# Banded attention inside a mixed layer: the low part of q on all 128 rows, and the softmax division on GpSimd

## The chip, the cores and the metric

One Trainium2 chip, one core. The metric is the device time of one execution in microseconds (us). TensorE is called PE below, its weight loads PEld, VectorE DVE, ScalarE ACT, GpSimd POOL, SyncE SP.

## The reference, cut to what matters

The whole block is a norm, an input projection, a linear recurrence beside a banded attention, an output projection, a cross attention over 256 memory rows, and a routed mixture of 32 experts. The change lies in the banded attention alone, which works on 2048 tokens, 8 heads of 64, each chunk of 64 queries seeing its own and the 8 chunks before:

```python
scores = jnp.einsum('bnqhd,bnkhd->bhnqk', qc, kb, preferred_element_type=jnp.float32)
scores = scores * (ATT_HEAD_DIM ** -0.5) + rel_bias_band(rel_bias).astype(jnp.float32)[None, :, None]
scores = jnp.where(valid[None, None, :, None, :], scores, NEG_INF)
probs = jax.nn.softmax(scores, axis=-1).astype(v.dtype)
out = jnp.einsum('bhnqk,bnkhd->bnqhd', probs, vb)
```

## The kernel before, in words

`front` (L646) computes the first half of the block, `phase2` the cross attention and the routing, `moe` the experts. `front` runs over 4 column groups `c` (two heads each) and, inside, over 4 blocks `t` of 512 tokens: 16 steps. All matrix products are done on pairs: each operand is split into a rounded part and the rest, and `mm3` (L54, L56 to L58) issues three matmuls for one product.

One call of `step` (L363) makes five projections of a block, in the order xr, xg, q, k, v (`run(0)` to `run(4)`; `proj`, L354, 24 matmuls of 128x512 each). After each 12 matmuls it calls `fill(i)`, i from 0 to 9, which runs the pieces of work that hang in slot i. Between the projections stands the recurrence: two gate products, a chain of ACT and DVE operations, and at its end the product `yr` (L425), its store (L426), its square (L561), the addition to a partial sum loaded from memory (L565) and the store of that (L566), these five on POOL.

The pieces in the slots are the attention of the step before (`attention`, L452). It has 8 units: 2 heads times 4 query tiles j of 128 queries. A unit's `scores` (L477) hangs in slot i, its `transp` (L501) in slot i+3, and for every second unit `out` (L516) in slot i+5; the last ones spill over into the slots 0 to 2 of the next step, `done` (L541) among them, which stores the attention's output and squares it on POOL.

In `scores` a unit's 640 keys lie in two parts of n1 and n2 columns, one from the block before and one from this block; in the first block of a column group there is only the second part, of 128 to 512 columns. For each part two matmuls add into the score tile `sc`: L486 with `qhh`, the rounded q twice on 128 rows, against `kst`, which holds rounded k on rows 0 to 63 and the rest of k on rows 64 to 127; and L487 with `qlo`, the rest of q on 64 rows, against the first 64 rows of `kst`. Then DVE adds the bias and takes the maximum (L490), ACT takes the exponential with its sum (L495), DVE the reciprocal of the sum (L497) and the product of the row with it (L498). `transp` turns the result on PE (L510) into `ptp`, from which ACT (L513) and DVE (L514) make the pair `PT`; `out` multiplies it with v (L534). `sc` and `ptp` have one buffer each.

`qhh` and `qlo` are made in `step` from the projection's PSUM tile `pq`: for each of two heads two ACT copies (L435, L436) and one DVE operation (L437). The projections share two PSUM buffers (`psA`), so the v projection (`run(4)`) writes where the q projection stood. Both engines read `pq`, and in the trace the second head's first copy waits for the first head's L437, of whose output it reads nothing.

The framework orders the instructions of each engine when the program is built; where the trace's order differs from the code's, that is its doing. POOL's queue also holds, in the last block of a column group, the splitting of the next group's weights (L342, L343), and in the first column group half of the splitting of h (L162).

Of the kernel before, what the change touches and what calls it, by code (L numbers as in the profile page):

```python
# [11 lines left out]
F32R = mybir.dt.float32r  # L12
# [4 lines left out]
ALU = mybir.AluOpType  # L17
# [9 lines left out]
TB = 512  # L27
# [18 lines left out]
def f32(ap):  # L46
    return ap.bitcast(F32)


class K:  # L50
# [312 lines left out]
    def step(self, c, t, st, wts, gh, gl, fill, h):  # L363

        nc = self.nc
        pt2 = self.pt2
        T2 = lambda name, dt=F32: pt2.tile([P, TB], dt, name=name, tag="t2")
        cnt = [0]

        def run(g):  # L370
            r = None
            for r in self.proj(wts[g], h):
                fill(cnt[0])
                cnt[0] += 1
            return r

        pxr = run(0)
        xre = self.p2.tile([P, TB + 3], F32, name="xre")
        if t == 0:
            nc.vector.memset(xre[:, 0:3], 0.0)  # L380
        else:
            nc.vector.tensor_copy(xre[:, 0:3], st["xre"][:, TB:TB + 3])
        nc.scalar.copy(xre[:, 3:], pxr)
        st["xre"] = xre
        cw = lambda i: self.col("convw", c * 4 + i)
        xc = T2("xc")
        nc.scalar.activation(xc, pxr, AF.Identity, scale=cw(3), bias=self.col("convb", c))
        for i in range(3):
            nc.vector.scalar_tensor_tensor(xc, xre[:, i:i + TB], cw(i), xc, op0=ALU.mult, op1=ALU.add)
        xch = T2("xch", F32R)  # L390
        xcl = T2("xcl", F32R)
        nc.scalar.copy(xch, xc)
        nc.vector.tensor_sub(xcl, xc, f32(xch))
        pxg = run(1)
        xg = T2("xg_half")
        nc.scalar.mul(xg, pxg, 0.5)
        th = []
        for gi in range(2):
            pg = self.psM.tile([P, TB], F32, name="pg", tag="m")
            self.mm3(pg, gh[:, gi], gl[:, gi], xch, xcl, True, True)  # L400
            tt = T2(f"th{gi}")
            nc.scalar.activation(tt, pg, AF.Tanh, scale=0.5, bias=self.hb[:, 4 * gi + c:4 * gi + c + 1])
            th.append(tt)
        kc_ = self.Kc[:, c:c + 1]
        av = T2("av")
        nc.scalar.activation(av, th[0], AF.Exp, scale=kc_, bias=kc_)
        tl_ = T2("tl")
        nc.scalar.activation(tl_, th[0], AF.Tanh, scale=kc_, bias=kc_)
        a2 = T2("a2")
        nc.scalar.activation(a2, av, AF.Square)  # L410
        g2 = T2("g2")
        nc.scalar.activation(g2, xg, AF.Square, scale=2.0)
        nc.vector.scalar_tensor_tensor(a2, a2, 1.0, tl_, op0=ALU.add, op1=ALU.mult)
        nc.vector.tensor_scalar(g2, g2, 0.044715, 1.0, op0=ALU.mult, op1=ALU.add)
        nc.vector.tensor_mul(g2, g2, xg)
        nc.scalar.activation(g2, g2, AF.Tanh, scale=2.0 * 0.7978845608028654)
        nc.scalar.activation(a2, a2, AF.Sqrt, scale=-0.25)
        nc.vector.scalar_tensor_tensor(xc, th[1], 1.0, xc, op0=ALU.add, op1=ALU.mult)
        nc.vector.tensor_mul(xc, xc, a2)
        hs = T2("hs")  # L420
        nc.vector.tensor_tensor_scan(hs, av, xc, 0.0 if t == 0 else st["h"][:, TB - 1:TB], op0=ALU.mult, op1=ALU.add)
        st["h"] = hs
        nc.vector.scalar_tensor_tensor(g2, g2, 1.0, xg, op0=ALU.add, op1=ALU.mult)
        yr = T2("yr")
        nc.gpsimd.tensor_tensor(yr, g2, hs, op=ALU.mult)  # L425
        nc.gpsimd.dma_start(out=self.yT[t][:, c], in_=yr)  # L426
        self.acc_sq(0, t, c, yr)

        pq = run(2)
        qst = []  # L430
        for hd in range(2):
            sl = slice(64 * hd, 64 * hd + 64)
            qhh = T2(f"qhh{hd}", F32R)
            qlo = pt2.tile([64, TB], F32R, name=f"qlo{hd}", tag="t2")
            nc.scalar.mul(qhh[0:64], pq[sl], 0.125)  # L435
            nc.scalar.mul(qhh[64:128], pq[sl], 0.125)  # L436
            nc.vector.scalar_tensor_tensor(qlo, pq[sl], 0.125, f32(qhh[0:64]), op0=ALU.mult, op1=ALU.subtract)  # L437
            qst.append((qhh, qlo))
        st["q"] = qst
        pk = run(3)  # L440
        for hd in range(2):
            sl = slice(64 * hd, 64 * hd + 64)
            kt = self.r3.tile([P, TB], F32R, name=f"kst{hd}")
            nc.scalar.copy(kt[0:64], pk[sl])
            nc.vector.tensor_sub(kt[64:128], pk[sl], f32(kt[0:64]))
            st[("k", t, hd)] = kt
        pv = run(4)
        vt = T2("vt")
        nc.scalar.copy(vt, pv)
        st["vt"] = vt  # L450

    def attention(self, c, t, st, bias):  # L452

        nc = self.nc
# [17 lines left out]
        def dims(j):  # L472
            n1 = 0 if t == 0 else (4 - j) * P
            n2 = (j + 1) * P
            return n1, n2, n1 + n2

        def scores(hd, j):  # L477
            qhh, qlo = qst[hd]
            qs = slice(j * P, (j + 1) * P)
            n1, n2, n = dims(j)  # L480
            sc = self.psS.tile([P, 1024], F32, name="sc")
            parts = [(sc[:, 512:512 + n2], kcur[hd][:, 0:n2])]
            if n1:
                parts.append((sc[:, 512 - n1:512], kprev[hd][:, j * P:TB]))
            for o, kk in parts:
                nc.tensor.matmul(o, qhh[:, qs], kk, start=True, stop=False)  # L486
                nc.tensor.matmul(o, qlo[:, qs], kk[0:64], start=False, stop=True)  # L487
            pr = self.r4.tile([P, 640], F32, name="st")
            mx = self.sm.tile([P, 1], F32, name="mx")
            nc.vector.tensor_tensor_reduce(pr[:, 0:n], sc[:, 512 - n1:512 + n2], bias[hd][:, 640 - n:640], 1.0, -3e38,  # L490
                                           op0=ALU.add, op1=ALU.max, accum_out=mx)
            nm = self.sm.tile([P, 1], F32, name="nm")
            nc.vector.tensor_scalar_mul(nm, mx, -1.0)  # L493
            ls = self.sm.tile([P, 1], F32, name="ls")
            nc.scalar.activation(pr[:, 0:n], pr[:, 0:n], AF.Exp, bias=nm, accum_out=ls)  # L495
            rl = self.sm.tile([P, 1], F32, name="rl")
            nc.vector.reciprocal(rl, ls)  # L497
            nc.vector.tensor_scalar_mul(pr[:, 0:n], pr[:, 0:n], rl)  # L498
            live[(hd, j)] = pr

        def transp(hd, j):  # L501
# [45 lines left out]
        for i, (hd, j) in enumerate(units):  # L547
            slots[i].append(lambda hd=hd, j=j: scores(hd, j))
            slots[i + 3].append(lambda hd=hd, j=j: transp(hd, j))
            if j % 2 == 1:  # L550
                slots[i + 5].append(lambda hd=hd, j=j: out(hd, j // 2))
# [542 lines left out]
    def moe(self):  # L1094
        nc, tc, a = self.nc, self.tc, self.a
        with ExitStack() as ctx:
# [259 lines left out]
            def unit(blks, ahead=(), last=None):  # L1356
# [40 lines left out]
                if not one:  # L1397
                    def mid(q):
                        if q == 1:
                            htrans(blks[0])  # L1400
                        step(1)
                        w.split()
                    hmid(blks[1], gu(blks[1], u, mid))
                    down(blks[0], d, put, lambda: (step(1), w.split()), False)
                    step(1)
                else:
                    w.split(2)
# [187 lines left out]
```

## Time and profile before

| what | value |
|---|---|
| device time, median of 3 runs | 2418.55 us (2418.11 to 2421.62) |
| the profiled execution | 2420.44 us |
| its span, first to last instruction | 2418.7 us |
| PE busy | 2298.4 us, 95% |
| DVE busy | 1572.8 us, 65% |
| ACT busy | 1351.3 us, 56% |
| POOL busy | 478.7 us, 20% |

The profile's page gives busy times and the costliest groups of instructions over the whole span. Its slices of the span show how busy each engine is over time, and the clock granted to TensorE. Busy time of PE is modelled for pipelined matmuls (a matmul's row lasts longer than the distance to the next one), so how fast PE works is read from the starts of its matmuls in the timeline.

### The profile page before, as it was taken

How to read it: one execution, taken by the hardware profiler on the slowest of the kernel's cores; microseconds unless marked ns; L12 is line 12 of the kernel's file. 1: busy time of each engine (PE TensorE's matmuls, PEld its weight loads, DVE VectorE, ACT ScalarE, POOL GpSimd, SP SyncE). 2: the span in 40 equal slices, each digit the busy share in tenths (PEclk: the TensorE clock that was granted, in tenths of full speed). 3: DMA queues.
4: the chain of work that ended last, by engine and by line, in shares of the span. 5: the costliest groups of instructions: out<-in, count | busy, mean ns of one | idle time of the engine just before them, and what ended most of it. 6: DMA issues, size and time to landing. Idle time of an engine off the chain costs nothing. (4 is left out here: it accounts for less than half of the span.)

```text
span 2418.7 us, 33205 instructions
## 1 busy us (share of the span) xinstructions
PE 2298.4 (95%) x11312; PEld 1868.2 (77%) x11312; DVE 1572.8 (65%) x3072; ACT 1351.3 (56%) x2300; POOL 478.7 (20%) x500
## 2 busy tenths in 40 slices
PE   8999999999999999999999999699999999999993
PEld 7766777787777778887888888577888777877782
DVE  7668766766776775435444444676777777777774
ACT  7677556555655664324343333466666667666654
POOL 1333521321241220000111111111212112121120
PEclk9999999999999999999999999799999999999997
DMA  8865642443334344633111111688998999989967
GB/s 329 297 233 177 216 156 105 144 176 121 133 125 167 121 141 140 200 109 131 53 64 60 62 53 60 230 277 292 301 309 281 307 298 297 310 275 307 298 207 307
DMA packets 160961, 475.83 MB, mean 197 GB/s; under 512 B 25393, under 2 KB 40370, under 8 KB 159506
## 3 DMA queue, kind: packets, MB, share of 16 engines
q1 hardware_dynamic: 129186, 369.92, 43.3%
q0 software_dynamic: 30448, 99.54, 13.5%
q10 hardware_dynamic: 1152, 4.19, 0.6%
q8 instruction: 90, 1.47, 0.2%
q14 instruction: 85, 0.70, 0.1%
HBM read 379.57 MB, written 98.99 MB: 198 GB/s over the span
## 5 line engine op out<-in xcount | busy, mean ns | idle before, releaser
L1141 DVE TENSOR_TENSOR w_hl<-w_raw,w_hl 128x1024 fp32r<-128x1024 f32 x384 | 458.9, 1216 | 120.3 <-ACT w_hl L1140 118.4
L1140 ACT CAST w_hl<-w_raw 128x1024 fp32r<-128x1024 f32 x384 | 388.9, 1049 | 143.9 <-DMA w_raw<-in_up_dram 35.0
L1209 PE MATMUL pg<-w_hl,xh 128*128 128x512 f32 x1120 | 355.9, 399 | 1.1 <-ACT xh L1198 1.1
L56 PE MATMUL pp<-h_hl,w_hl 128*128 128x512 f32 x640 | 264.4, 415 | 2.0 <-ACT h_hl L161 1.0
L58 PE MATMUL pp<-h_hl,w_hl 128*128 128x512 f32 x640 | 251.7, 394 | 2.9 <-DVE w_hl L340 2.9
L57 PE MATMUL pp<-h_hl,w_hl 128*128 128x512 f32 x640 | 251.9, 394 | 1.6 <-DVE h_hl L162 0.9
L1209 PEld LDWEIGHTS pg<-w_hl,xh 128*128 128x128 f32 x1120 | 205.6, 189 | 42.6 <-ACT xh L1198 1.5
L1209 PE MATMUL pg<-w_hl,xl 128*128 128x512 f32 x560 | 219.9, 393 | 0.0
L1272 PE MATMUL py<-w_hl,hth 128*128 128x512 f32 x560 | 143.9, 400 | 23.0 <-ACT hth L1255 23.0
L1259 POOL DMA_INDIRECT acc_d<-ys,ti x46 | 85.3, 1854 | 385.2 <-ACT ys L1276 371.6
L56 PEld LDWEIGHTS pp<-h_hl,w_hl 128*128 128x128 f32 x640 | 120.3, 188 | 37.9 <-issue 9.2
L1272 PEld LDWEIGHTS py<-w_hl,hth 128*128 128x128 f32 x560 | 106.3, 192 | 51.6 <-ACT hth L1255 29.7
L58 PEld LDWEIGHTS pp<-h_hl,w_hl 128*128 128x128 f32 x640 | 120.5, 188 | 30.5 <-DVE w_hl L340 3.3
L495 ACT ACTIVATE st<-st,nm 128x640 f32<-128x640 f32 (+4 forms) x128 | 97.3, 761 | 80.2 <-DVE nm L493 79.6
L57 PEld LDWEIGHTS pp<-h_hl,w_hl 128*128 128x128 f32 x640 | 120.9, 189 | 25.3 <-POOL h_hl L162 2.5
L514 DVE TENSOR_TENSOR PT<-ptp,PT 128x640 fp32r<-128x640 f32 (+4 forms) x128 | 94.1, 735 | 51.5 <-ACT PT L513 51.1
L1209 PEld LDWEIGHTS pg<-w_hl,xl 128*128 128x128 f32 x560 | 105.5, 188 | 23.2
L490 DVE CUSTOM_DVE_ANT_0 st<-sc,bias 128x640 f32<-128x640 f32 (+4 forms) x128 | 94.3, 737 | 38.5 <-PE sc L487 36.7
L1178 POOL DMA_INDIRECT xs<-h_d,ti x48 | 59.4, 1238 | 294.3 <-PE px L1189 129.1
L56 PE MATMUL sc<-At,xh 128*128 128x512 f32 x256 | 103.7, 405 | 1.3 <-ACT xh L830 1.3
L498 DVE TENSOR_SCALAR st<-st,rl 128x640 f32<-128x640 f32 (+4 forms) x128 | 102.7, 802 | 3.1
L1209 PE MATMUL pg<-w_hl,xr 128*128 128x512 f32 x416 | 102.4, 393 | 0.0
(389 smaller groups left out, 5151.8 us busy)
## 6 DMA issues: line engine op xcount, KB each, us to landing
w_raw<-in_gate_dram SPq DMA_DIRECT2D x128, 512.0 KB
w_raw<-in_up_dram SPq DMA_DIRECT2D x128, 512.0 KB
w_raw<-in_down_dram SPq DMA_DIRECT2D x128, 512.0 KB
h_hl<-hT SPq DMA_DIRECT2D x96, 512.0 KB
hT<-h_hl POOLq DMA_DIRECT2D x32, 512.0 KB, 6.4
w_raw<-in_w_in_dram SPq DMA_DIRECT2D x40, 256.0 KB
xr<-in_x_dram SPq DMA_DIRECT2D x32, 256.0 KB
xt<-in_xT_dram SPq DMA_DIRECT2D x32, 256.0 KB
```

Of the source, the lines that this page charges most:

```text
L56: mm(ps, lh, rh, start=start, stop=False)
L57: mm(ps, lh, rl, start=False, stop=False)
L58: mm(ps, ll, rh, start=False, stop=stop)
L490: nc.vector.tensor_tensor_reduce(pr[:, 0:n], sc[:, 512 - n1:512 + n2], bias[hd][:, 640 - n:640], 1.0, -3e38, op0=ALU.add, op1=ALU.max, acc ...
L495: nc.scalar.activation(pr[:, 0:n], pr[:, 0:n], AF.Exp, bias=nm, accum_out=ls)
L498: nc.vector.tensor_scalar_mul(pr[:, 0:n], pr[:, 0:n], rl)
L514: nc.vector.tensor_sub(PT[:, 1, s0:s0 + nb], src, f32(PT[:, 0, s0:s0 + nb]))
L1140: nc.scalar.copy(wt[:, 0], raw)
L1141: nc.vector.tensor_sub(wt[:, 1], raw, f32(wt[:, 0]))
L1209: nc.tensor.matmul(pg, x[:, k], wt[:, l, cs], start=(k == 0 and i == 0), stop=(k == KC - 1 and i == np_ - 1))
L1259: nc.gpsimd.indirect_dma_start(out=self.acc_d, in_=ys[0:b.n], in_offset=None, compute_op=op, out_offset=bass.IndirectOffsetOnAxis(ap=b.ti[ ...
L1272: nc.tensor.matmul(o, h[:, k], m[k][:, l, nn * TB:(nn + 1) * TB], start=(j == 0), stop=(j == len(ps) - 1))
```

## The change

The low part of q is written to both halves of 128 rows, by two DVE operations for a head where there was one, in the order ACT, DVE, ACT, DVE. The second matmul of a score part contracts over 128 rows, with the whole of `kst`; so the product of the low part of q with the low part of k, which was left out, is added. The product of the exponentials with the reciprocal of their sum moves from DVE to POOL.

```diff
             qhh = T2(f"qhh{hd}", F32R)
-            qlo = pt2.tile([64, TB], F32R, name=f"qlo{hd}", tag="t2")
-            nc.scalar.mul(qhh[0:64], pq[sl], 0.125)
-            nc.scalar.mul(qhh[64:128], pq[sl], 0.125)
-            nc.vector.scalar_tensor_tensor(qlo, pq[sl], 0.125, f32(qhh[0:64]), op0=ALU.mult, op1=ALU.subtract)
+            qlo = T2(f"qlo{hd}", F32R)
+            for o in (slice(0, 64), slice(64, 128)):
+                nc.scalar.mul(qhh[o], pq[sl], 0.125)
+                nc.vector.scalar_tensor_tensor(qlo[o], pq[sl], 0.125, f32(qhh[0:64]), op0=ALU.mult, op1=ALU.subtract)
...
                 nc.tensor.matmul(o, qhh[:, qs], kk, start=True, stop=False)
-                nc.tensor.matmul(o, qlo[:, qs], kk[0:64], start=False, stop=True)
+                nc.tensor.matmul(o, qlo[:, qs], kk, start=False, stop=True)
...
             nc.vector.reciprocal(rl, ls)
-            nc.vector.tensor_scalar_mul(pr[:, 0:n], pr[:, 0:n], rl)
+            nc.gpsimd.tensor_scalar(pr[:, 0:n], pr[:, 0:n], rl, None, op0=ALU.mult)
```

## Rows read from the trace of the kernel before

**Rows 1.** Busy time of the engines by stretch; each engine's number of instructions in brackets.
```profile
core 0: us, PE busy (x) PEld busy (x) DVE busy (x) ACT busy (x) POOL busy (x), PEclk, DMA share, GB/s
150.00:407.40 257.40, 250.13 (x1198) 193.58 (x1198) 188.41 (x402) 165.38 (x321) 84.69 (x100) 0.99 0.50 180
407.40:850.00 442.60, 442.60 (x2184) 348.75 (x2182) 301.98 (x636) 257.80 (x467) 121.92 (x129) 1.00 0.39 137
...
457.70:508.00 50.30, 50.30 (x253) 39.56 (x252) 35.11 (x70) 28.43 (x50) 25.27 (x27) 1.00 0.46 160
```

**Rows 2.** The score matmuls of L487: durations in ns, counts, first and last start, forms.
```profile
L487 PE MATMUL sc<-kst,qlo x224: 322/436/792, 150.2 to 920.1; 64*128 64x128 f32 x32, 64*128 64x384 f32 x32, 64*128 64x256 f32 x24, 64*128 64x512 f32 x24
```

**Rows 3.** Timeline of PE, one unit of two parts: start us, duration us, instruction.
```profile
424.01 0.73 PE L510 MATMUL ptp<-ident,st 128*128 128x128 f32 x5
424.49 0.42 PE L486 MATMUL sc<-kst,qhh 128*128 128x384 f32 x1
...
425.84 0.50 PE L56 MATMUL pp<-h_hl,w_hl 128*128 128x512 f32 x1
426.18 0.39 PE L57 MATMUL pp<-h_hl,w_hl 128*128 128x512 f32 x1
426.41 0.40 PE L58 MATMUL pp<-h_hl,w_hl 128*128 128x512 f32 x1
...
428.93 0.71 PE L510 MATMUL ptp<-ident,st 128*128 128x128 f32 x5
...
430.51 0.50 PE L56 MATMUL pp<-h_hl,w_hl 128*128 128x512 f32 x1
```

**Rows 4.** Timeline of PE, two units of one part, of 128 and of 512 columns.
```profile
561.01 0.30 PE L486 MATMUL sc<-kst,qhh 128*128 128x128 f32 x1
...
561.25 0.32 PE L487 MATMUL sc<-kst,qlo 64*128 64x128 f32 x1
...
561.50 0.50 PE L56 MATMUL pp<-h_hl,w_hl 128*128 128x512 f32 x1
...
561.84 0.39 PE L57 MATMUL pp<-h_hl,w_hl 128*128 128x512 f32 x1
...
572.48 0.48 PE L486 MATMUL sc<-kst,qhh 128*128 128x512 f32 x1
572.89 0.49 PE L487 MATMUL sc<-kst,qlo 64*128 64x512 f32 x1
573.31 0.50 PE L56 MATMUL pp<-h_hl,w_hl 128*128 128x512 f32 x1
573.65 0.40 PE L57 MATMUL pp<-h_hl,w_hl 128*128 128x512 f32 x1
```

**Rows 5.** The page's row of the division: busy us, mean ns of one.
```profile
L498 DVE TENSOR_SCALAR st<-st,rl 128x640 f32<-128x640 f32 (+4 forms) x128 | 102.7, 802 | 3.1
```

**Rows 6.** Timeline of DVE in the same step as rows 3.
```profile
402.59 0.56 DVE L498 TENSOR_SCALAR st<-st,rl 128x640 f32<-128x640 f32 x1
...
421.40 1.62 DVE L498 TENSOR_SCALAR st<-st,rl 128x640 f32<-128x640 f32 x1
...
426.88 0.69 DVE L437 SCALAR_TENSOR_TENSOR qlo<-pp,qhh 64x512 fp32r<-64x512 f32 x1
```

**Rows 7.** Groups of POOL by form: busy us, mean ns of one, idle us before.
```profile
L425 POOL TENSOR_TENSOR yr<-g,hs 128x512 f32<-128x512 f32 x16 | 21.0, 1312 | 159.6 <-DVE nm L493 99.2 <-DVE rl L497 49.4 <-DVE g L423 10.9
L342 POOL CAST w_hl<-w_raw 128x512 fp32r<-128x512 f32 x30 | 19.6, 672 | 0.0
```

**Rows 8.** Timeline of POOL in that step, the recurrence's first and last operation.
```profile
421.38 1.29 POOL L425 TENSOR_TENSOR yr<-g,hs 128x512 f32<-128x512 f32 x1 [12.91 <-DVE nm L493]
...
426.39 0.56 POOL L566 DMA_DIRECT2D q<-sq  x1 [0.30 <-POOL sq L565]
```

**Rows 9.** Timeline of ACT in that step: xg, and the second head's copy of q.
```profile
407.43 0.60 ACT L396 ACTIVATE xg_half<-pp 128x512 f32<-128x512 f32 x1 [0.97 <-PE pp L58]
...
425.65 0.60 ACT L435 ACTIVATE qhh<-pp 64x512 fp32r<-64x512 f32 x1 [1.07 <-DVE qlo L437]
```

## The prediction

> **What bounds the kernel now.** I read the busy times by stretch first. From 407.4 to 850 us, nine steps of the loop that the change sits in, PE is busy for all 442.6 us, while DVE has 302, ACT 258 and POOL 122 us; even in a step that also splits weights POOL has 25.3 of 50.3 us. Between 150 and 407 us PE is idle for 7.3 us of 257.4. The clock is full (1.00, 0.99) [rows 1]. So PE sets the pace, and a saving counts if it shortens the distance between PE's starts.
>
> Then the score lines: 224 matmuls of L487, one for each of L486, from 150 to 920 us, with 64 rows of weights where L486 has 128 [rows 2, 3]. 224 pairs are 96 units with two parts and 32 with one.
>
> Then PE's timeline around one unit of each kind. Projection matmuls of 512 columns start 0.23 us apart (426.18, 426.41), and five transposes of 128 columns about 0.115 apart, (0.73 less the 0.27 of the last) / 4, where 0.27 is what one such row lasts; I take it as the price of a 128-column matmul with new weights. The score matmuls stand further apart: four of 384, 384, 256 and 256 columns take 1.35, and the projection matmul after them is followed only after 0.34 [rows 3]. With one part: 0.24, 0.25, 0.34 for 128 columns, 0.41, 0.42, 0.34 for 512 [rows 4]. What differs from the plain ones is that the number of rows changes, from 128 to 64 and back: each change costs some 0.1 to 0.2 us, and both changes fall on every pair.
>
> **The change part by part. (a) Scores on 128 rows.** No change of rows is left. Price after: 0.23 for 512 columns, 0.115 for 128, between them by proportion 0.15 for 256 and 0.19 for 384, which is generous.
> - Unit 384+256: before 425.84 - 424.49 = 1.35, plus 0.34; after 2 x (0.19 + 0.15) + 0.23 = 0.91. Saves 0.78.
> - One part of 512: 0.41 + 0.42 + 0.34 - 3 x 0.23 = 0.48. One part of 128: 0.24 + 0.25 + 0.34 - (2 x 0.115 + 0.23) = 0.37. Mean of the one-part units 0.43.
> - Unit 512+128: 0.48 + 0.37, less the 0.11 that follows a unit once and not twice: 0.74.
>
> 96 x 0.76 + 32 x 0.43 = 73 + 14 = **87 us off PE**. It all lies on PE's own path.
>
> **(b) The division leaves DVE.** 102.7 us of DVE go [rows 5]. In a step where PE bounds that is worth nothing by itself. Where PE is idle before 407 us it may be worth up to 7.3 us [rows 1]; I take 3 and keep 0 and 7. A quicker PE also needs `ptp` emptied sooner; that DVE no longer stands 1.62 us in a division ahead of it [rows 6] is why I cost that at nothing. Without that relief PE could wait for the 1.5 us that it gains over two units, once a step.
>
> **(c) The division arrives on POOL.** No row shows POOL multiplying by a per-row scalar. Nearest rows: a cast of 512 elements, one input, 0.67 us; a product of two tensors, 1.31 us [rows 7]. For 640 elements that makes 0.84 and 1.64. One tensor is read, so I take the cast's rate, 0.9. Eight of them are 7 us a step, on an engine that has half a step free even in its fullest steps. The load fits; the order is the question. `yr` and what follows hold POOL from 421.38 to 426.95, with waits for their own predecessors [rows 8]. In the order of the code the fifth unit's division stands behind all that and ends at 426.95 + 0.9 = 427.85; its transposes start at 428.93 [rows 3], so today 1.1 us would be left. But four units have passed on PE since the chain that leads to `yr` was started (L396, 407.43 [rows 9]), each 0.76 shorter after the change: PE is there 3.0 us sooner, and waits 1.9. The transposes of successive units are 4.9 us apart (424.01, 428.93 [rows 3]), over 4 after the change, so the later divisions don't wait again. Over 15 steps: 29 us. Against it: the builder orders the engines by what is ready, and if the division is put ahead of L426 to L566 there is no wait. Ends 0 and 29; between, 14.
>
> The GPSIMD Engine Reference of the Trainium skill (section 4.1, Engine selection) speaks against this part: elementwise work belongs on VectorE, being about 2x slower on GPSIMD for two inputs, though near line rate for one. At twice DVE's undisturbed 0.56 us [rows 6] the division would take 1.1, and the sum would be 15 x 0.2 = 3 us worse.
>
> **(d) Two more DVE operations a head-pair, in a longer relay.** 32 x 0.69 = 22 us on DVE, hidden as in (b): DVE still loses 80 us. But all eight readers of `pq` now take turns, ACT, DVE, ACT, DVE; before, six did with three changes of engine, the last ending at 426.88 + 0.69 = 427.57 [rows 6]. The v projection needs that PSUM buffer at 430.51 [rows 3]: 2.9 us spare. Three units passed on PE since `pq` was complete, so PE comes 2.3 us sooner and 0.6 is left. The relay grows by 2 x 0.69 and four changes of engine (the gap where ACT waited for DVE was 1.07 at 425.65 [rows 9], most of it DVE's own queue; 0.1 to 0.3 without), some 2 to 2.5; two divisions that stood ahead of its first DVE operation are gone, some 1.5 back. So about 0.5 us a step, 8 us. Ends 0 and 3 us a step, 45. While the relay runs, ACT stands in front of its next exponentials and PE's copies; these have three slots of room before the transposes.
>
> **Sum.** -87 - 3 + 14 + 8 = -68. The profiled execution took 2420.44, so 2352; the median of the runs lies 1.9 lower: **2350 us**. The rest of the kernel starts earlier by as much and is not touched.
>
> **The rivals.**
> - *Nothing is given back* (both order costs 0, DVE's relief full): 2418.5 - 87 - 7 = 2324. For it: PE is the only engine near its limit, and the order in the trace is already not the code's.
> - *Most is given back in the two queues*: 29 in POOL and some 30 in the relay, 2418.5 - 87 + 59 = 2390. For it: the margins, 1.1 and 2.9 us, are smaller than what PE gains before them. Against: the division's units before the fifth, and everything else, have more.
> - *The stall isn't the change of rows* but belongs to the score matmuls (their tile, their operands): then nothing leaves PE, and 2418 plus what (c) costs today, next to nothing. Against: the plain L56 after the pair is stretched too, and only its neighbour's row count differs.
> - *Slower: POOL's multiplication is far dearer than its cast.* Place: the wait of the transposes for the division. The saving is 0.76 x 8 = 6 us a step, so it decides from a wait of 6 us: the division would have to take 0.9 + 4, about 5 us. Then eight would be 40 us a step, and with the 25.3 of the steps with weights POOL would exceed the step and bound. At 5.5 us: a wait of some 6.5 in 15 steps and 20 more in three of them, 2418.5 - 87 + 98 + 60 = 2490. Nothing in the rows makes it likely beyond the missing price. A DVE division that began together with `yr` on POOL took 1.62 instead of 0.56 [rows 6, 8], so POOL's new work may hold back DVE's other operations too, but eight times 0.9 us a step can't cost more than what DVE loses with the divisions, 102.7 / 16 = 6.4 a step, by more than 1 us.
>
> **How the numbers follow.** Forecast as above, 2335 to 2370: 0.55. Nothing given back: 0.17. Most given back: 0.20. Not the rows: 0.03. Slower: 0.05. From 2318 (full saving, with a few us of error in the prices by column) to 2392 holds the first three nearly whole; a little is left out on each side, with the last two. What a measurement here can tell from no change is about 0.2%, 5 us: faster by more 0.92, within 0.03, slower 0.05.
>
> **What would show it.** Right: L487 in the form 128*128, score matmuls 0.12 to 0.23 apart, and the steps about 45 to 46 us instead of 50.3. Division rows on POOL of 0.8 to 1.0 us. If (c) holds, PE waits before L510 for POOL; if (d), before the first L56 of the v projection, for DVE's L437. Wrong: score matmuls as far apart as before; division rows over 1.7 us; PE's wait before L510 of more than 3 us in each step, or DVE rows that grow while POOL divides.

## The result, and the profile after

The median is 2388.3 us (2384.7 to 2391.9, four runs) against 2418.3 of the kernel before beside it, a ratio of 0.9873 [0.9852, 0.9893]. So the change gains 30 us, where 68 were forecast. The profiled execution took 2390.94 us.

The page of the kernel after, its busy times and the division's row, which answers to [rows 5]:

```profile
span 2389.2 us, 33573 instructions
...
PE 2236.6 (94%) x11312; PEld 1861.8 (78%) x11312; DVE 1524.5 (64%) x2976; ACT 1351.9 (57%) x2300; POOL 697.4 (29%) x628
...
L498 POOL TENSOR_SCALAR st<-st,rl 128x640 f32<-128x640 f32 (+4 forms) x128 | 220.0, 1719 | 181.9 <-DVE rl L497 167.9
```

PE is busy for 62 us less (2298.4 before), but the execution's span is only 29.5 us shorter. The division, 102.7 us on DVE, is 220.0 us on POOL. Its rows by form in the kernel after (busy us, mean ns of one), beside POOL's prices in [rows 7]:

```profile
L498 POOL TENSOR_SCALAR st<-st,rl 128x640 f32<-128x640 f32 x96 | 182.5, 1901 | 140.7 <-DVE rl L497 126.9 <-DVE nm L493 6.5 <-PE pav L534 4.3
...
L498 POOL TENSOR_SCALAR st<-st,rl 128x512 f32<-128x512 f32 x8 | 12.6, 1572 | 9.3 <-DVE rl L497 9.2
```

The division takes 1.90 us for 640 columns: not the cast's rate that was taken (0.9), and above the upper end (1.64, the product of two tensors).

PE's timeline after, around a unit of 384 and 256 columns as in [rows 3]:

```profile
418.72 0.42 PE L486 MATMUL sc<-kst,qhh 128*128 128x384 f32 x1
418.97 0.34 PE L487 MATMUL sc<-kst,qlo 128*128 128x384 f32 x1
419.15 0.28 PE L486 MATMUL sc<-kst,qhh 128*128 128x256 f32 x1
419.27 0.28 PE L487 MATMUL sc<-kst,qlo 128*128 128x256 f32 x1
419.39 0.39 PE L56 MATMUL pp<-h_hl,w_hl 128*128 128x512 f32 x1
419.62 0.40 PE L57 MATMUL pp<-h_hl,w_hl 128*128 128x512 f32 x1
...
```

The four score matmuls take 419.39 - 418.72 = 0.67 us and the next projection matmul is followed after 0.23, where 1.35 and 0.34 stood before: 0.79 us less, and 0.78 was worked out. So the unit behaves as forecast, and the missing time is elsewhere.

To find it I cut out the stretch from the first to the last copy of v (ACT, L449), 15 steps of the loop, and read PE's busy time in it for both kernels; [rows 1] has the columns. The kernel before:

```profile
149.10:873.10 724.00, 714.69 (x3492) 559.50 (x3492) 509.39 (x1068) 440.16 (x816) 216.56 (x235) 1.00 0.42 152
```

The kernel after, the whole stretch and one episode inside it:

```profile
157.30:851.00 693.70, 656.98 (x3483) 553.36 (x3481) 459.21 (x969) 438.54 (x811) 416.17 (x354) 0.98 0.44 157
498.30:508.00 9.70, 9.11 (x46) 7.26 (x44) 6.78 (x9) 7.85 (x14) 8.95 (x9) 1.00 0.29 95
508.00:512.00 4.00, 1.11 (x6) 1.15 (x7) 4.00 (x8) 2.91 (x4) 0.38 (x1) 0.84 0.00 0
512.00:514.10 2.10, 2.10 (x8) 1.91 (x8) 1.30 (x2) 1.00 (x3) 0.00 (x0) 0.50 0.00 0
```

PE's busy time falls by 57.7 us, but its idle time grows from 9.3 to 36.7. And the mean granted clock is 0.98 instead of 1.00: after six of PE's seven gaps of more than 1.8 us between starts comes a stretch at a granted clock of 0.50 (the 1.2 GHz level), as in the last line; after the seventh, of 2.9 us at 460, none. Added up over the trace's records of the clock, such stretches are 27.3 us of these 15 steps, against 6.8 before. In them a matmul of 512 columns follows the one before after 0.43 us instead of 0.23, so about half of the 20.5 us between the two, some 10, is work that takes longer (an estimate). So PE's work got lighter by some 57.7 + 10 = 68 us, and 10 + 27 of that went into slow clock and waiting: 30 are left.

The waits of PE for the transposes (150 to 880 us; who waited, for whom: us in all, times, longest; "issue" where the profile shows nothing that was waited for), kernel before:

```profile
PEld ptp L510 <- DVE PT L514: 4.8, 4, 2.7
...
PE ptp L510 <- DVE PT L514: 3.7, 3, 2.4
```

Kernel after:

```profile
PE ptp L510 <- DVE PT L514: 20.3, 11, 3.5
PEld ptp L510 <- issue: 17.6, 15, 3.9
PEld ptp L510 <- POOL st L498: 11.4, 6, 3.1
...
PEld pp L56 <- DVE qlo L437: 3.8, 5, 1.3
```

(PE and PEld can stand in the same gap, so the rows are not to be added.) Five of the six longest gaps lie in two places. The first is in the last block of a column group, where POOL begins to split weights. POOL's timeline of the kernel after, and DVE's beside it:

```profile
452.86 1.19 POOL L342 CAST w_hl<-w_raw 128x512 fp32r<-128x512 f32 x2
454.00 2.54 POOL L343 TENSOR_TENSOR w_hl<-w_raw,w_hl 128x512 fp32r<-128x512 f32 x2
...
458.21 1.88 POOL L498 TENSOR_SCALAR st<-st,rl 128x640 f32<-128x640 f32 x1
...
454.71 2.40 DVE L413 SCALAR_TENSOR_TENSOR a<-a,tl 128x512 f32<-128x512 f32 x1 [1.77 <-ACT a L410]
...
459.47 0.81 DVE L514 TENSOR_TENSOR PT<-ptp,PT 128x640 fp32r<-128x640 f32 x1
```

The division ends at 460.09, behind 5.4 us of weight splitting, and PE's transposes start at 460.43. But L514, which empties `ptp` for them, ends only at 460.28, because DVE's L413 ahead of it takes 2.40 us; it takes 0.69 in the kernel before, all sixteen times (691 to 693 ns). So two things hold PE there, and they end within 0.2 us of each other. The same stands at 281 and at 644 us (at 281 it is L414 that is long, 1.52 us). The second place is in the step after, the first of the next column group, in which POOL splits the last of the five weight tiles; there it is DVE alone that is held up. DVE's, POOL's and PE's timeline, kernel after:

```profile
502.82 1.18 POOL L342 CAST w_hl<-w_raw 128x512 fp32r<-128x512 f32 x2
503.97 2.54 POOL L343 TENSOR_TENSOR w_hl<-w_raw,w_hl 128x512 fp32r<-128x512 f32 x2
504.23 3.60 DVE L413 SCALAR_TENSOR_TENSOR a<-a,tl 128x512 f32<-128x512 f32 x1 [1.67 <-ACT a L410]
506.50 1.89 POOL L498 TENSOR_SCALAR st<-st,rl 128x640 f32<-128x640 f32 x1
507.02 0.39 PE L58 MATMUL pp<-h_hl,w_hl 128*128 128x512 f32 x1
507.75 0.91 DVE L414 TENSOR_SCALAR g<-g 128x512 f32<-128x512 f32 x1
508.59 0.81 DVE L490 CUSTOM_DVE_ANT_0 st<-sc,bias 128x640 f32<-128x640 f32 x1
509.93 0.81 DVE L514 TENSOR_TENSOR PT<-ptp,PT 128x640 fp32r<-128x640 f32 x1
510.88 1.30 PE L510 MATMUL ptp<-ident,st 128*128 128x128 f32 x5 [3.48 <-DVE PT L514]
```

L413 reads two tensors from SBUF. Here it stands for 3.60 us instead of 0.69, while POOL goes from the splitting into the division without a pause. L490 and L514 queue behind it on DVE, and PE, which started its last matmul at 507.02, starts again at 510.88, at half the clock. The next column group has the same at 695 us; at 829 us, where POOL splits the output projection's weights, it is the same with L413 at 2.18 us.

### The profile page after: what moved, and what is told of

The parts are those of the page before. It is cut to its first block, busy times and chain, and to the rows that moved or that the text cites. A ratio compares the mean times of both kernels' runs of the same rounds, so it can differ in the third digit from the quotient of the medians.

```text
span 2389.2 us, 33573 instructions
## 1 busy us (share of the span) xinstructions
PE 2236.6 (94%) x11312; PEld 1861.8 (78%) x11312; DVE 1524.5 (64%) x2976; ACT 1351.9 (57%) x2300; POOL 697.4 (29%) x628
## 3 DMA queue, kind: packets, MB, share of 16 engines
q0 software_dynamic: 30448, 99.54, 13.7%
## 5 line engine op out<-in xcount | busy, mean ns | idle before, releaser
L498 POOL TENSOR_SCALAR st<-st,rl 128x640 f32<-128x640 f32 (+4 forms) x128 | 220.0, 1719 | 181.9 <-DVE rl L497 167.9
L56 PE MATMUL pp<-h_hl,w_hl 128*128 128x512 f32 x640 | 259.5, 407 | 3.2 <-DVE qlo L437 2.8
L58 PEld LDWEIGHTS pp<-h_hl,w_hl 128*128 128x128 f32 x640 | 122.6, 192 | 30.7 <-DVE w_hl L340 3.3
L57 PEld LDWEIGHTS pp<-h_hl,w_hl 128*128 128x128 f32 x640 | 122.9, 192 | 28.2 <-POOL h_hl L162 4.6
L56 PEld LDWEIGHTS pp<-h_hl,w_hl 128*128 128x128 f32 x640 | 123.4, 193 | 27.6 <-DVE qlo L437 3.8
L514 DVE TENSOR_TENSOR PT<-ptp,PT 128x640 fp32r<-128x640 f32 (+4 forms) x128 | 94.2, 736 | 61.6 <-ACT PT L513 60.5
L510 PE MATMUL ptp<-ident,st 128*128 128x128 f32 x560 | 86.2, 280 | 26.2 <-DVE PT L514 23.2
L490 DVE CUSTOM_DVE_ANT_0 st<-sc,bias 128x640 f32<-128x640 f32 (+4 forms) x128 | 93.8, 733 | 25.9 <-PE sc L487 25.2
L56 PE MATMUL sc<-At,xh 128*128 128x512 f32 x256 | 103.7, 405 | 1.4 <-ACT xh L830 1.4
```

What stands on the lines that cost most here:

```text
L56: mm(ps, lh, rh, start=start, stop=False)
L57: mm(ps, lh, rl, start=False, stop=False)
L58: mm(ps, ll, rh, start=False, stop=stop)
L498: nc.gpsimd.tensor_scalar(pr[:, 0:n], pr[:, 0:n], rl, None, op0=ALU.mult)
L510: nc.tensor.transpose(ptp[:, b * P:(b + 1) * P], pr[:, b * P:(b + 1) * P], self.ident)
L514: nc.vector.tensor_sub(PT[:, 1, s0:s0 + nb], src, f32(PT[:, 0, s0:s0 + nb]))
```

## The experiments

Each was run four to twelve times beside the kernel before on the same chip (2419.8 to 2420.9 us): e1, e2, e4 and e5 on one chip, e7 to e10 on a second, e11 to e14 on a third, so across these groups the ratios are the surer comparison. The table holds each ratio, and for the 15 steps the length, PE's busy time and the difference, PE's idle time. The 15 steps are those of one profiled execution. Their length is the sure number; busy against idle is rough, and short waits seem to count as busy (e4 and e10 have the same matmuls and the same 6.8 us at a clock of 0.50, and yet 652.1 and 643.7 us busy). e8 stands further below.

| kernel | median us | ratio | 15 steps | PE busy | PE idle |
|---|---|---|---|---|---|
| before | 2418.3 | 1 | 724.0 | 714.7 | 9.3 |
| after | 2388.3 | 0.9873 [0.9852, 0.9893] | 693.7 | 657.0 | 36.7 |
| e1, scores only | 2384.9 | 0.9851 [0.9831, 0.9870] | 694.5 | 654.1 | 40.4 |
| e2, division only | 2425.8 | 1.0026 [1.0015, 1.0038] | 733.2 | 720.3 | 12.9 |
| e4, e1 + short relay | 2367.3 | 0.9784 [0.9766, 0.9802] | 675.8 | 652.1 | 23.7 |
| e5, grouped rows | 2391.9 | 0.9875 [0.9855, 0.9894] | 698.3 | 686.6 | 11.7 |
| e7, after + short relay | 2373.0 | 0.9815 [0.9798, 0.9831] | 683.1 | 652.6 | 30.5 |
| e9, halves by DMA | 2392.8 | 0.9896 [0.9879, 0.9913] | 699.6 | 656.2 | 43.4 |
| e10, no division | 2409.8 (see there) | 0.9951 [0.9938, 0.9965] | 654.8 | 643.7 | 11.1 |
| e11, POOL in blocks 0, 1 | 2360.0 | 0.9746 [0.9726, 0.9766] | 672.4 | 647.2 | 25.2 |
| e12, division on ACT | 2391.8 | 0.9882 [0.9864, 0.9900] | 693.0 | 656.3 | 36.7 |
| e13, output divided | 2366.3 | 0.9778 [0.9762, 0.9795] | 674.4 | 655.4 | 19.0 |
| e14, POOL in blocks 2, 3 | 2377.6 | 0.9826 [0.9809, 0.9843] | 681.5 | 653.6 | 27.9 |

### The two parts of the change, each alone

**e1: the kernel after, with the division back on DVE.**

```diff
-            nc.gpsimd.tensor_scalar(pr[:, 0:n], pr[:, 0:n], rl, None, op0=ALU.mult)
+            nc.vector.tensor_scalar_mul(pr[:, 0:n], pr[:, 0:n], rl)
```

> The changed kernel with the division back on DVE. Theory A (the division on POOL, 1.72 us on the mean and queued behind POOL's other work, eats the gain): about 2418 - 72 = 2346 us, since PE's score matmuls and their neighbours got 72 us shorter. Theory B (the longer relay of ACT and DVE on q eats it): stays near 2388. Theory C (ACT and DVE can't follow a quicker PE, wherever the division is): 2380 to 2388, with PE's waits before L510 for L514 as large as in the changed kernel.

**e2: the kernel before, with only the division on POOL** (the same two lines, the other way round).

> The kernel before with only the division moved to POOL. Theory A: slower than before, by up to the 42 us that are missing, 2430 to 2460 us; less if the slower PE leaves POOL more time. Theories B and C: within 5 us of 2418, since DVE loses 103 us of work and PE bounds.

Moving the division alone costs 5.6 us, less than theory A and a little more than B and C allowed. Taking it back off POOL in the kernel after gives only 3.4, and the intervals of e1 and after overlap. So the move to POOL is not what eats most of the gain: the change of the scores alone, with the division where it was, brings 35 us of the forecast 87, and PE idles as long as after (40.4 against 36.7), though in other places: none of e1's gaps between starts is over 2.4 us, and only 13.7 us of its 15 steps are at the clock of 0.50. Something in the scores' part makes PE wait as well.

### Is it the change of rows?

**e5: the kernel before, with the two matmuls over 128 rows of a unit ahead of the two over 64.** In the 96 units of two parts, two changes of rows are left of four; nothing else moves.

```diff
             for o, kk in parts:
                 nc.tensor.matmul(o, qhh[:, qs], kk, start=True, stop=False)
+            for o, kk in parts:
                 nc.tensor.matmul(o, qlo[:, qs], kk[0:64], start=False, stop=True)
```

> The kernel before, but in a unit of two parts both L486 come before both L487, so the number of rows changes twice a unit and not four times. If the cost lies in the change of rows: 96 units x 2 changes x 0.17 us = 33 us faster, about 2385. If it belongs to the 64-row matmuls or the score tile: 2418, unchanged.

2420.2 to 2391.9: 28 us for 192 changes fewer, 0.147 us each, with no instruction removed. All 448 changes (4 x 96 + 2 x 32) would be 66 us by that. The starts in the trace give more: a unit of 384 and 256 columns with the projection matmul behind it takes 1.27 us in e5 (median), against 1.68 in the kernel before and 0.89 after, so 0.20 for each change, and not all of it reaches the end of the kernel. The kernel after alternates the two kinds of matmul as the kernel before does, with 128 rows throughout, and has no stall; so it isn't the alternation. This small reordering alone gains about as much as the whole change.

### The longer relay

The relay is the row of ACT copies and DVE operations that read q's PSUM tile in turns.

**e4: e1 with both ACT copies of a head ahead of both DVE operations**, so that the engines change places once a head and not three times.

```diff
             for o in (slice(0, 64), slice(64, 128)):
                 nc.scalar.mul(qhh[o], pq[sl], 0.125)
+            for o in (slice(0, 64), slice(64, 128)):
                 nc.vector.scalar_tensor_tensor(qlo[o], pq[sl], 0.125, f32(qhh[0:64]), op0=ALU.mult, op1=ALU.subtract)
```

> As the kernel with the scores alone, division on DVE, but for each head both ACT copies before both DVE operations. Theory A: the same as the scores alone, within 5 us. Theory B: 30 to 40 us faster than the scores alone, near 2350. If the relay costs what the prediction said, 8 us faster at most.

The order of four instructions a head is worth 17.6 us (2384.9 to 2367.3); the two intervals do not meet. That is half of what theory B expected and twice what the prediction's price allowed. (The builder, which orders each engine by what is ready, moved other instructions with them, so what is shown is the worth of this edit with all that follows from it.) The waits of e1, 150 to 880 us:

```profile
DVE PT L514 <- ACT PT L513: 43.0, 31, 4.0
...
ACT qhh L436 <- DVE qlo L437: 37.3, 27, 4.6
...
PE ptp L510 <- DVE PT L514: 22.4, 21, 2.0
...
PEld ptp L510 <- DVE PT L514: 18.3, 15, 2.2
...
PEld pp L56 <- DVE qlo L437: 3.9, 4, 2.4
```

The same of e4 (its lines are one further down):

```profile
DVE PT L515 <- ACT PT L514: 35.3, 32, 2.6
...
ACT qhh L436 <- DVE qlo L438: 16.3, 12, 5.3
...
PE ptp L511 <- DVE PT L515: 12.8, 16, 1.6
...
PEld ptp L511 <- DVE PT L515: 8.2, 7, 1.6
...
PEld pp L56 <- DVE qlo L438: 3.1, 6, 1.5
```

In e1 the ACT copies of q wait 37.3 us for DVE's operation ahead of them; in e4 that falls to 16.3. While ACT stands there, its copy of `ptp` (L513) comes late, then DVE's L514, and PE waits for L514 at the next transposes. One such place in e1:

```profile
416.92 0.59 ACT L436 ACTIVATE qhh<-pp 64x512 fp32r<-64x512 f32 x1 [2.74 <-DVE qlo L437]
...
417.92 0.69 ACT L513 CAST PT<-ptp 128x640 fp32r<-128x640 f32 x1
...
420.33 0.81 DVE L514 TENSOR_TENSOR PT<-ptp,PT 128x640 fp32r<-128x640 f32 x1
...
421.20 0.77 PE L510 MATMUL ptp<-ident,st 128*128 128x128 f32 x5 [1.55 <-DVE PT L514]
```

L513 starts here 2.70 us after the transposes that it empties (415.22); in e4 it starts 0.78 us after them (409.05 and 409.83), and the next transposes don't wait. The v projection, whose PSUM buffer the relay holds, hardly waits in either kernel (3.9 and 3.1 us).

**e7: the kernel after with the same short relay**, the division on POOL.

> The changed kernel, division on POOL, with both ACT copies of a head before both DVE operations. The scores alone went from 2385 to 2367 us by this. If the relay's cost and the division's are separate, 2388 - 18 = 2370 us. If POOL's late divisions are the real limit once the relay is short, it stays over 2380.

It is near the 2370 of separate costs: 15.3 us less than after. In the two profiled executions 10.6 us of it lie in the 15 steps, where PE is both less busy (4.4) and less idle (6.2), and 5.3 ahead of the first v copy, of which 4.6 are there before the first copy of q and so are not the relay's. In the kernel after, the copies of q wait only 13.6 us for DVE, so the path that e1 and e4 show is not as plain to read in this pair. Against e4 it is 5.6 us slower: the price of the division on POOL once more, now with the relay out of the way (the two intervals overlap by a little, e2's price is the surer one).

**e9: the second halves by DMA.** One ACT copy and one DVE operation a head, then two transfers on POOL's queue; the division on DVE.

```diff
-            for o in (slice(0, 64), slice(64, 128)):
-                nc.scalar.mul(qhh[o], pq[sl], 0.125)
-                nc.vector.scalar_tensor_tensor(qlo[o], pq[sl], 0.125, f32(qhh[0:64]), op0=ALU.mult, op1=ALU.subtract)
+            nc.scalar.mul(qhh[0:64], pq[sl], 0.125)
+            nc.vector.scalar_tensor_tensor(qlo[0:64], pq[sl], 0.125, f32(qhh[0:64]), op0=ALU.mult, op1=ALU.subtract)
+            nc.gpsimd.dma_start(out=f32(qhh[64:128]), in_=f32(qhh[0:64]))
+            nc.gpsimd.dma_start(out=f32(qlo[64:128]), in_=f32(qlo[0:64]))
```

> Scores on 128 rows, division on DVE, and for each head one ACT copy and one DVE operation from PSUM, the second halves of both tiles filled by a DMA from the first. The relay has four readers of PSUM in place of eight, ACT loses 19 us and DVE 22 us against the scores alone. Theory B (the readers of q in turns hold ACT and DVE, and so the copies that empty the transposes' tile): as fast as the short relay or faster, 2350 to 2367 us. If the relay only mattered by its length up to the v projection's buffer: 2367.

A miss: 2392.8 us, and the most idle time of PE in the table (43.4). From its first to its last instruction the relay takes 4.7 us (median of the steps), against 8.3 in e1 and 7.0 in e4, and yet the transposes wait longer. The trace shows where: of the 23.8 us that the 15 steps take longer than e4's, 20.8 lie in three of them, each the first step of a column group. Around the start of each a division on DVE, 0.55 us in the median, stands for 4.35 us (at 294), 5.79 (at 473) or 5.78 (at 657) while POOL splits weights, with L515 behind it:

```profile
473.56 5.79 DVE L499 TENSOR_SCALAR st<-st,rl 128x640 f32<-128x640 f32 x1
...
480.57 1.33 PE L511 MATMUL ptp<-ident,st 128*128 128x128 f32 x5 [3.97 <-DVE PT L515]
```

The transfers' issue adds 30 us to POOL's queue (245.6 against 216.0 us busy in the 15 steps), so POOL splits at another time than in e4; that this is what brings the splitting beside the division was not tried apart. So e9 says little on the relay itself.

### What the division costs, wherever it stands

**e10: e7 without the division and its reciprocal.**

```diff
-            rl = self.sm.tile([P, 1], F32, name="rl")
-            nc.vector.reciprocal(rl, ls)
-            nc.gpsimd.tensor_scalar(pr[:, 0:n], pr[:, 0:n], rl, None, op0=ALU.mult)
```

> Scores on 128 rows, short relay, and the reciprocal and the division left out (rows are not divided by their sums). It takes the division off both engines. If DVE's division is what keeps the short relay's 2367 us from the 2346 that PE's saving allows: 2346 to 2352. If ACT's own queue holds PE back: 2362 or more.

The total cannot be compared, since from the last v copy to the end it takes 1604.0 us, against 1545.6 before; presumably because rows that are not divided change what the routing sees later. Its 15 steps can:

```profile
152.10:806.90 654.80, 643.67 (x3490) 545.98 (x3491) 429.04 (x856) 439.08 (x814) 213.17 (x235) 0.99 0.47 166
```

69.2 us shorter than before, PE 71.0 us less busy and idle for 11.1 us, about what it was before. So PE's lighter work can be had nearly whole, when the division is gone. With it, the same 15 steps cost 21.0 us more on DVE (e4) and 28.3 more on POOL (e7).

**e8: the kernel after, POOL multiplying by a constant** in place of the reciprocal.

```diff
-            nc.gpsimd.tensor_scalar(pr[:, 0:n], pr[:, 0:n], rl, None, op0=ALU.mult)
+            nc.gpsimd.tensor_scalar(pr[:, 0:n], pr[:, 0:n], 0.5, None, op0=ALU.mult)
```

> The changed kernel with POOL multiplying by the number 0.5 in place of the per-row reciprocal: the rows are not divided by their sums. It measures POOL's operation. If the per-row scalar makes it dear, the 128x640 row falls from 1.90 us to the cast's rate, about 0.84, and the time by up to 20 us. If the operation itself is dear, the row stays near 1.9 and the time near 2388.

Its total (2436.7 us) can't be compared either, for the same reason. The row of the operation for 640 columns (busy us, mean ns of one):

```profile
L498 POOL TENSOR_SCALAR st<-st 128x640 f32<-128x640 f32 x96 | 179.5, 1870 | 170.6 <-ACT st L495 167.7 <-issue 1.3 <-PE pp L58 1.1
```

1.87 us against 1.90 in the kernel after: the operation itself is dear on POOL, whether its factor is one number or one per row.

**e12: e7 with the division on ACT.**

```diff
-            nc.gpsimd.tensor_scalar(pr[:, 0:n], pr[:, 0:n], rl, None, op0=ALU.mult)
+            nc.scalar.mul(pr[:, 0:n], pr[:, 0:n], rl)
```

> Scores on 128 rows, short relay, the division on ACT (some 0.8 us for 640 elements, 128 times). It takes no port that POOL and DVE share. If only the waits between DVE and POOL hold PE back: 2350 to 2358. If ACT's own queue, which also makes the copies that empty the transposes' tile, is as tight: 2370 to 2390.

2391.8 us, just above what was expected for ACT's queue being as tight: dearer than on either of the others (38.2 us over e10 in the 15 steps), though ACT is busy for only 440 of the 724 us before, less than DVE (509).

**e13: the attention's output divided instead.** The rows stay undivided; two small products on PE spread the reciprocals over the tile of `pav`, and DVE multiplies 64x256 of output by them, for two units at a time.

```diff
-            nc.gpsimd.tensor_scalar(pr[:, 0:n], pr[:, 0:n], rl, None, op0=ALU.mult)
+            live["rl", hd, j] = rl
...
+            for b in range(2):
+                self.bcast_rows(pav4[:, 2 + b], live["rl", hd, 2 * pr + b][:, 0:1])
...
+            nc.vector.tensor_mul(yo, yo, pav4[own, 2:4])
```

> Scores on 128 rows, short relay, no division of the rows: the attention's output is multiplied by the reciprocals instead, two 128x128 transposes on PE (0.23 us) and one DVE operation on 64x256 elements (0.42 us) for two units. PE gets 15 us more, DVE loses 103 us and gets 27. With the division left out the 16 steps' stretch was 69 us shorter than before, with the division on DVE 48; so 2350 + 15 - some of it hidden = 2352 to 2362. If the relief of DVE isn't what counts: 2367 + 15 = 2382.

2366.3 us, level with e4 and above the 2352 to 2362 that were expected. It takes the division out of the chain ahead of the transposes (idle 19.0 against 23.7) and pays for that on PE (655.4 busy against 652.1). PE still idles for 8 us more than in e10, so being out of the chain is not the whole of what e10 gains; how much of the division's cost comes from its place in the chain, and how much from the time it takes on its engine, is not separated.

### Where POOL's work does harm

**e11: e7 with the division on POOL only for the blocks t = 0 and 1, on DVE for the others. e14: the reverse.** A block's attention runs in the step after. POOL splits four of the next group's weight tiles in the step t = 3, and the fifth in the first step of that group, t = 0 (POOL's L342 and L343 run there too, as at 503 us above). So in e11 POOL divides in the steps t = 1 and 2 alone, in which it splits nothing, and in e14 in the steps 3 and 0 alone.

```diff
-            nc.gpsimd.tensor_scalar(pr[:, 0:n], pr[:, 0:n], rl, None, op0=ALU.mult)
+            if t < 2:
+                nc.gpsimd.tensor_scalar(pr[:, 0:n], pr[:, 0:n], rl, None, op0=ALU.mult)
+            else:
+                nc.vector.tensor_scalar_mul(pr[:, 0:n], pr[:, 0:n], rl)
```

> Scores on 128 rows, short relay; the division on POOL for the first two blocks of a column group, whose attention runs while POOL splits no weights, on DVE for the other two. Theory D (POOL's division costs where POOL also splits weights: DVE operations with two inputs from SBUF stand until POOL pauses, L413 3.6 us in place of 0.7, and PE waits behind them): faster than with all divisions on DVE (2367 us) or all on POOL (2373), 2358 to 2364. If the place of the division matters equally in all steps: between the two, 2367 to 2373.

> The reverse: POOL divides for the last two blocks of a column group, DVE for the first two. Theory D: slower than the split the other way by 8 to 16 us, 2372 to 2380, with the long L413 rows back. If the place matters equally in all steps: as the other split.

2360.0 against 2377.6 us, both within theory D's ranges, with the same number of divisions on POOL (half of e11's are the narrow ones of first blocks, 128 to 512 columns). The row of L413 in e11 (shortest, median, longest, ns):

```profile
L413 DVE SCALAR_TENSOR_TENSOR a<-a,tl x16: 674/692/1241, 125.1 to 798.0; 128x512 f32<-128x512 f32 x16
```

In e14:

```profile
L413 DVE SCALAR_TENSOR_TENSOR a<-a,tl x16: 691/693/3608, 121.5 to 803.5; 128x512 f32<-128x512 f32 x16
```

The 3.6 us rows are there in e14 and gone in e11. The length of the steps shows the same for all kernels. From one v copy to the next, in the third column group (us):

| kernel | t = 0 | t = 1 | t = 2 | t = 3 |
|---|---|---|---|---|
| before | 50.3 | 41.5 | 48.5 | 50.3 |
| e10, no division | 44.6 | 38.7 | 42.9 | 45.2 |
| e4, on DVE | 46.1 | 39.3 | 44.0 | 46.5 |
| e7, on POOL | 49.7 | 38.8 | 43.1 | 49.4 |
| e11, POOL in blocks 0, 1 | 46.2 | 38.7 | 43.1 | 46.5 |
| e14, POOL in blocks 2, 3 | 49.7 | 39.3 | 43.9 | 47.7 |
| e1, alternating relay, DVE | 47.6 | 41.0 | 45.4 | 47.0 |
| after, alternating relay, POOL | 51.0 | 40.2 | 43.8 | 50.0 |

In the steps without splitting the division on POOL costs 0.1 to 0.2 us over no division at all, less than on DVE (0.6 and 1.1), though its rows are more than three times as long. In the two steps with splitting it costs 4 to 5 us (1.0 to 5.1 over all groups), against 1.3 and 1.5 on DVE. The alternating relay costs something in every step: 0.5 to 1.7 us (e1 over e4, after over e7).

e11 is 7.3 us below e4, which divides on DVE alone; their intervals just touch, so this last gain is likely rather than sure. e11 is the best version that was run, 28 us below the kernel after, and it beats both kernels.

## Why the prediction was wrong

Faster by more than 0.2% was right, and 2388 lies inside the range; but of the 68 us only 30 came. The step that failed is (b) first of all: what a quicker PE asks of `ptp` was costed at nothing because DVE would be free. In the steps in which POOL splits weights DVE isn't free, and the division on POOL costs 28.3 us in all, where (b) and (c) together had 11. The rival "most is given back in the two queues" named the time, 2390, by other terms than those that came.

**(a) Right in mechanism, near in size.** The form of L487, the distances and the saving of a unit are as worked out, and e5 shows that it is the change of rows. Over the 15 steps PE's work falls by 71.0 us (e10), some 76 for 16 steps, where 87 were summed. Of the 11 between, about half are prices: by the medians of the trace a unit of 512 and 128 columns saves 0.68 (0.74 was taken) and a unit of one part 0.37 (0.43); the rest is not located. The step "it all lies on PE's own path" holds only while the others keep up: the 15 steps get 69.2 us shorter in e10, and 29.5 in e1.

**(b) The cover that held in half of the steps only.** "That DVE no longer stands 1.62 us in a division ahead of it is why I cost that at nothing" failed. In the steps in which POOL splits nothing it held: from the second column group on, POOL's division costs at most 0.2 us a step there (e7 over e10). In the steps t = 3 and t = 0 DVE lost its division, but other operations stood as long in its place, L413 for 2.2 to 3.6 us, with L514, which empties `ptp`, behind them. In these steps lie 25.1 of the 28.3 us that the division on POOL costs in the 15 steps (e7 over e10). Left on DVE, the division costs 21.0 us (e4 over e10): the relief was needed, and it was not to be had on a POOL that splits weights beside it. The sentence kept as the alternative, "PE could wait for the 1.5 us that it gains over two units, once a step", is 15 x 1.5 = 22, and near in number to the division on DVE; it gave no price to the division on POOL.

**(c) The price, and the place.** The price was taken from the wrong row: 1.90 us and not 0.9, above the upper end. The place was wrong as well: behind `yr` the builder put a division between L561 and L565, and PE did not wait for it. This is POOL's timeline of the kernel after, in the step of the unit shown above:

```profile
419.89 1.05 POOL L561 TENSOR_TENSOR sq<-yr 128x512 f32<-128x512 f32 x1
420.91 1.89 POOL L498 TENSOR_SCALAR st<-st,rl 128x640 f32<-128x640 f32 x1
422.78 1.26 POOL L565 TENSOR_TENSOR sq<-sq,sqp 128x512 f32<-128x512 f32 x1
```

What did hold the division is the weight splitting, at 281, 460 and 644 us, where PE waits 2.5 to 2.7 us for it and for L514, which ends with it. The sum of (b) and (c), 14 - 3 = 11, made the move worth while against the 22 of the alternative in (b); measured, the move costs 3.4 (e1 to after) or 5.6 (e4 to e7, and e2).

One sentence reasoned wrongly, and the net hid it. It stands in the slower rival: POOL's new work "can't cost more than what DVE loses ... by more than 1 us". It compared busy times of an average step, with eight divisions of 0.9 us where they take 1.9. On the average the net is indeed below 1 us a step (5.6 / 16). But in the third group it is a small gain in two steps and some 3 us lost in each of the other two (e7 against e4), and what counts there is a DVE operation that is held for 2.2 to 3.6 us in a step in which POOL is full, with the operation that frees `ptp` behind it. The prediction's last paragraph had named such rows as a sign of being wrong ("DVE rows that grow while POOL divides").

The Trainium skill's GPSIMD Engine Reference (section 4.1, Engine selection) puts an operation with one input near line rate on GPSIMD. The trace disagrees: 1.90 us for what DVE does in 0.56 undisturbed [rows 6].

**(d) Mis-sized and misplaced.** 8 us were taken; the relay costs 17.6 (e1 to e4), and 10.6 of the 15 steps between after and e7. The prediction's own terms gave less than 8: the relay's net growth, 2 to 2.5 less 1.5, stands against 0.6 us that were left, so at most 0.4 us a step and not 0.5. The place named, the first L56 of the v projection, waits 3.8 us in all. In e1 it is ACT, standing in the relay, whose late copies of `ptp` keep PE from its transposes; the text named that ("these have three slots of room") and costed it at nothing. For the pair after and e7 this path is argued, not shown.

**Nothing priced the clock.** The waits above are of 2.5 to 3.5 us at a time, and after most of them the granted clock is 0.50 for some us; that is the 10 us worked out above. There is more of it where PE's gaps in the splitting steps are long: 27.3 us of the 15 steps in after, 23.9 in e7 and 27.3 in e9, but 6.8 in e4, e10 and e11.

Set together, for the 15 steps: -69.2 us without a division and with the short relay (e10), +21.0 for the division on DVE (e4), +7.3 for its move to POOL (e7), +10.6 for the alternating relay (after), in all -30.3. The prediction had -87 for the first, +11 for the division on POOL, where 28.3 came, and +8 for the relay. So of the 38 us between forecast and result some 18 lie in the first term (whose 87 held 16 steps), 17 in the division and 3 in the relay. Before and behind the 15 steps the two kernels differ by 8.2 us lost and 7.4 gained, which nearly cancel.

The 8.2 us are lost ahead of the first v copy of after (157.3 against 149.1). That is not the relay: the first copy of q is already 6.3 us late (143.7 against 137.4). At 127.7 PE starts again after a gap of 2.4 us (1.5 before), in the preparation of the cross attention, and from 128.4 to 135.2 the granted clock is 0.50; neither before nor e7 has such a gap or such a stretch there. e8, which differs from after only in the factor of the division, has the same stretch, and its first v copy at 156.9; the other kernels lie between 148.2 and 152.9. Why these two wait longer there was not tried, nor was taking the weight splitting off POOL.

## What to carry to other kernels

When the bounding engine gets lighter, walk the whole chain that feeds it again, at its new pace: work that was hidden has a cost from the moment the slack is used up, and moving a step to an engine with time to spare pays only in the steps in which that engine has it. Where two engines take turns on one tile, group each engine's instructions: a turn that comes late makes what is queued behind it late as well. And before work goes to POOL, look at what else POOL has in that step and at the DVE operations beside it: give it the steps in which it is free, not all of them.

## What the runs showed of the hardware that was not expected

- On POOL a product of 512 columns with one scalar a row takes 1.57 us, more than its product of two tensors of the same size (1.31 [rows 7]), though it reads one tensor less; a constant factor hardly helps (1.87 against 1.90 us for 640 columns, e8).
- One DVE operation with two SBUF inputs stood for 3.60 us, across the end of POOL's splitting and into the division that followed without a pause. The GPSIMD Engine Reference of the Trainium skill (section 1, Specifications) says that GPSIMD's SBUF interfaces are shared with VectorE and contend with its instructions that run in a 2-port perf mode or have two SBUF inputs; the row agrees for two inputs, with 3.60 against 0.69. The division, which reads one tensor and a factor a row, was held on DVE as well: 4.68 us at 855 in the kernel before, and 5.79 in e9 while POOL split weights, against 0.55; in which mode it runs no run here shows.
- A change between 128 and 64 rows of weights on PE costs 0.20 us in the distance of starts and 0.147 in the kernel's time (e5), so a product over 64 rows between products over 128 is dearer than one that fills all 128.
- After a gap of 3.9 us in PE's starts (507.02 to 510.88) the granted clock was 0.50 for the matmuls that followed, and those of 512 columns came 0.43 us apart instead of 0.23, up to 514.1.
